# One-hot rows of the PEER gates: two tokens side by side in memory instead of four

## The chip, the core and the metric

The kernel runs on one core of a Trainium2 chip. The metric is the device time of one execution, in microseconds; the median of the runs shown counts. Every time below is from a run of this kernel or from one profiled execution of it.

TensorE (PE in the profile, its weight loads PEld) multiplies; VectorE (DVE) and ScalarE (ACT) do the elementwise work and empty the accumulators (PSUM banks, `bank` in the rows); GpSimd (POOL) helps; SyncE's queue (SPq) issues the transfers.

## The reference, cut to what matters

The network is a block with a recurrent mixer, a windowed attention and a mixture of experts, and behind it two layers of a second kind, each of which ends with PEER: 256 tokens, 16384 experts, eight heads that pick sixteen experts each. Only PEER is touched.

```python
def peer_ffn(x, wq, sub_keys, u_tab, v_tab):
    ...
    def block(xi):
        qv = (xi @ wq).reshape(B, PEER_BLOCK, PEER_HEADS, 2, half)
        s = jnp.einsum('bthpc,hpnc->bthpn', qv, sub_keys).astype(jnp.float32)
        top_s, top_i = lax.top_k(s, K)
        cand_s = (top_s[..., 0, :, None] + top_s[..., 1, None, :]).reshape(...)
        cand_i = (top_i[..., 0, :, None] * N_KEYS + top_i[..., 1, None, :]).reshape(...)
        best_s, best_j = lax.top_k(cand_s, K)
        expert = jnp.take_along_axis(cand_i, best_j, axis=-1)
        gate = jax.nn.softmax(best_s, axis=-1)
        act = jax.nn.gelu(jnp.einsum('btd,bthkd->bthk', xi, u_tab[expert]).astype(jnp.float32), approximate=False)
        return jnp.einsum('bthk,bthkd->btd', (gate * act).astype(xi.dtype), v_tab[expert])
```

An expert's number is n * 128 + m, two halves of 0 to 127. A token has 128 picks (8 heads of 16), each with a pair (n, m) and a gate.

## The kernel before

The kernel does not gather. For every token it computes gelu(u_e . x) of all 16384 experts and multiplies by a dense matrix of gates that is zero where an expert was not picked. `peer` has four parts.

*Queries and picks.* `pick` (line 2141) finds the picks of 128 tokens at a time. At its end (lines 2259 to 2262) TensorE transposes the four tables nn, mm, gh, gl (first half, second half, the gate in two float16 parts) into one PSUM bank, and ScalarE copies the bank into `picks`, float16, 128 picks on the partitions, as [4 tables, 256 tokens].

*Up.* `up` (line 2079) runs over 128 units of u. A unit is 128 experts: 24 matmuls of 256 columns in three float32r products (lines 418 to 420, `mm3`: high by high, low by high, high by low) into banks 0 to 2, then Gelu on ScalarE into B, [128, 128 units, 256 tokens]. Each unit's 512 KB arrive by a transfer on SyncE's queue; ScalarE splits off the high part (line 336), VectorE or GpSimd the low part (line 337, tile `wl`). While `pick` is busy on VectorE, units of `up` are put between its steps.

*Gating.* `gating` (line 2265) makes the gates, four tokens in a step, 64 steps in a layer. `hot` writes two float16 tiles of 128 x 1024 elements on VectorE. `e` (tile eq, line 2278) holds two one-hot tables: for each pick and each number 0 to 127, whether the pick's n (and m) is that number. `g` (tile gm, line 2279) is the one-hot of m multiplied by the gate's two parts. Then eight matmuls (line 2290), two for each token: weights are 128 numbers of one token of e, the moving columns 128 numbers of one token of g, summed over the 128 picks, so that a bank (of 3 to 6) gets the gates of 4 tokens. VectorE multiplies them into those units of B that are there (line 2292); for those that are still to come ScalarE stores the gates in B (line 2294), and `up` later applies them (lines 2086 to 2089). Both tiles have two buffers, and a step makes the tiles of the next one ahead.

*Down.* 128 units of v, matmuls of 512 columns (`down`, line 2119), accumulate in four banks.

Gating runs against `up`: `interleave` puts one step of the one behind one unit of the other, so that TensorE's queue holds 8 float16 matmuls and then 24 float32r ones, over and over. A scheduler in the framework sets each engine's final order from simulated times.

What the change touches is the order of the 1024 elements in a partition of eq and gm. Now the innermost index is the token, four side by side: the numbers 0, 1, 2, ... of one token stand 4 elements (8 bytes) apart, and that is the step with which TensorE reads both its weights and its columns at line 2290. VectorE reads `picks` in rows of four tokens, each repeated 128 times, and `iota16` (each number four times) in one run.

Of the kernel before, what the change touches and what calls it, by code (L numbers as in the profile page):

```python
# [12 lines left out]
F16 = mybir.dt.float16  # L13
U32 = mybir.dt.uint32
AF = mybir.ActivationFunctionType
OP = mybir.AluOpType
# [4 lines left out]
T = 256  # L21
# [319 lines left out]
def interleave(*gens):  # L341

    live = [[g, n] for g, n in gens]
    while live:
        for it in list(live):
            for _ in range(it[1]):
                try:
                    next(it[0])
                except StopIteration:
                    live.remove(it)  # L350
                    break
# [7 lines left out]
class Net:  # L359
# [1701 lines left out]
    def peer(self, l):  # L2061

        nc, tc, A, st = self.nc, self.tc, self.A, self.st
        with ExitStack() as es:
            pp = es.enter_context(tc.tile_pool(name="peer", bufs=1))
            B = pp.tile([128, 128, T], F32, name="B")
            picks = pp.tile([128, 4, T], F16, name="picks")
            hs = ExitStack()
            hp = hs.enter_context(tc.tile_pool(name="px", bufs=1))
            xh, xl = self.normal_t(hp, B[:, 64:72])  # L2070
            qT = B[:, 112:128].rearrange("p j t -> p (j t)").rearrange("p (j t) -> p j t", j=16)
            for j in range(16):
                ps = self.bank(0, 1)[:, :T]
                self.dense_t(ps, "wq", xh, xl)
                nc.scalar.copy(qT[:, j], ps)  # L2075

            at = dict(m=0, t=0)

            def up():

                for m in range(128):
                    ps = self.bank(0, 1, 2)[:, :T]
                    self.dense_t(ps, "pu", xh, xl)
                    t = at["t"]
                    if t < T:
                        nc.scalar.activation(B[:, m, t:], ps[:, t:], AF.Gelu)
                    if t:
                        nc.scalar.activation(ps[:, :t], ps[:, :t], AF.Gelu)
                        nc.vector.tensor_tensor(B[:, m, :t], B[:, m, :t], ps[:, :t], op=OP.mult)
                    at["m"] = m + 1  # L2090
                    yield

            ups = up()
            with tc.tile_pool(name="pk", bufs=1) as kp:
                st.pool_every = 3
                due = 0.0
                for us in self.pick(kp, l, B, qT, picks):
                    due += us
                    while due >= PICK_US:
                        due -= PICK_US  # L2100
                        next(ups)
            st.pool_every = 0
            with tc.tile_pool(name="pg", bufs=1) as pg:
                interleave((self.gating(pg, B, picks, at), 1), (ups, 1))
            st.pool_every = 0
            hs.close()
            pp = es.enter_context(tc.tile_pool(name="pv", bufs=1))
            acc = [self.ps[4 + b] for b in range(4)]
            self.settle(pp)
            parts = {}  # L2110

            def cut(m):
                parts[m] = [pp.tile([128, T], F32R, name=n, bufs=4) for n in ("gh", "gll")]
                self.split(*parts[m], B[:, m])

            cut(0)
            cut(1)

            def down(m, tt, gh, gl, wh, wl):
                t = slice(tt * 128, tt * 128 + 128)  # L2120
                for half in range(2):
                    c = slice(half * 512, half * 512 + 512)
                    ins = self.mm3(acc[tt * 2 + half], gh[:, t], gl[:, t], wh[:, c], wl[:, c], m == 0, m == 127)
                return ins

            for m in range(126):
                w = st.get("pv")
                cut(m + 2)
                for tt in range(2):
                    down(m, tt, *parts[m], *w)  # L2130
                del parts[m]
            st.hold = st.at + 2
            w = [st.get("pv") for _ in range(2)]

            down(126, 0, *parts[126], *w[0])
            with tc.issue_after(down(127, 0, *parts[127], *w[1]).ins):
                for j in range(2):
                    down(126 + j, 1, *parts[126 + j], *w[j])
            return [[(half, acc[tt * 2 + half]) for half in range(2)] for tt in range(2)]

    def pick(self, kp, l, B, qT, picks):
# [3 lines left out]
        nc, A = self.nc, self.A  # L2145
# [5 lines left out]
        def t(nm, shape, dt=F32, bufs=1):  # L2151
            if dt != F32:
                return kp.tile(shape, dt, name=nm, bufs=bufs)
            size = int(np.prod(shape[1:]))
            key = made.setdefault(nm, [used[0], 0])
            if not key[1]:
                used[0] += size * bufs
                assert used[0] <= 8192
            a = key[0] + key[1] % bufs * size
            key[1] += 1  # L2160
            ax = "abc"[:len(shape) - 1]
            return R[:, a:a + size].rearrange(f"p ({' '.join(ax)}) -> p {' '.join(ax)}", **dict(zip(ax, shape[1:])))
# [15 lines left out]
        for tt in range(2):  # L2178
# [32 lines left out]
            g = t("g", [128, 8, 16])  # L2211
# [17 lines left out]
            for h0 in range(0, 8, 4):  # L2229
                hs = slice(h0, h0 + 4)  # L2230
                big = [128, 4, 16, 15]
# [17 lines left out]
            for h0 in range(0, 8, 4):  # L2249
                big = [128, 16, 16]  # L2250
# [8 lines left out]
            pt = self.bank(3, 4)  # L2259
            for j, a in enumerate((nn, mm, gh, gl)):  # L2260
                nc.tensor.transpose(pt[:, j * 128:j * 128 + 128], a.rearrange("p h k -> p (h k)"), self.ident)
            nc.scalar.copy(picks[:, :, tt * 128:tt * 128 + 128], pt.rearrange("p (j t) -> p j t", j=4))
            yield 0.0

    def gating(self, pp, B, picks, at):


        nc = self.nc
        iota = pp.tile([128, 128, 4], F16, name="iota16")
        nc.vector.tensor_copy(iota, self.iota[:, :, None].to_broadcast([128, 128, 4]))  # L2270
        big = [128, 2, 128, 4]

        def hot(t0):

            e = pp.tile(big, F16, name="eq", bufs=2)
            g = pp.tile(big, F16, name="gm", bufs=2)
            of = lambda i: picks[:, i:i + 2, None, t0:t0 + 4].to_broadcast(big)
            nc.vector.tensor_tensor(e, iota[:, None].to_broadcast(big), of(0), op=OP.is_equal)  # L2278
            nc.vector.tensor_tensor(g, e[:, 1:2].to_broadcast(big), of(2), op=OP.mult)
            return e, g  # L2280

        made = {0: hot(0)}
        for t0 in range(0, T, 4):
            if t0 + 4 < T:
                made[t0 + 4] = hot(t0 + 4)
            e, g = made.pop(t0)
            ps = self.bank(3, 4, 5, 6).rearrange("p (t m) -> p m t", t=4)
            for j in range(4):
                for i in range(2):
                    nc.tensor.matmul(ps[:, :, j], e[:, 0, :, j], g[:, i, :, j], start=i == 0, stop=i == 1)  # L2290
            m, t = at["m"], slice(t0, t0 + 4)
            nc.vector.scalar_tensor_tensor(B[:, :m, t], B[:, :m, t], GATE_UNIT, ps[:, :m], op0=OP.mult, op1=OP.mult)
            if m < 128:
                nc.scalar.activation(B[:, m:, t], ps[:, m:], AF.Copy, scale=GATE_UNIT)
            at["t"] = t0 + 4
            yield
# [41 lines left out]
```

## Time and profile before

| | |
|---|---|
| median of 3 runs | 3211.7 us (3210.72 to 3220.12) |
| the profiled execution | 3216.49 us, its span 3214.7 us |
| granted TensorE clock, mean | 0.964 |
| TensorE busy | 3032.4 us, 94% of the span |
| VectorE, ScalarE, GpSimd busy | 2030.8, 1411.6, 374.5 us |
| gating, first layer | about 1405 to 1650 us of the span |
| gating, second layer | about 2589 to 2828 us |

A busy share is a mean over stages with different limits; what counts here is who is waited for in the two stretches of gating. A row of the timeline has start, length, engine, line, operation, what is written and read, and how many like it were merged; matmuls overlap, so the distance between starts tells what one costs, not its length. In the rows of one line, three numbers with slashes are the shortest, median and longest length in ns.

### The profile page before, as it was taken

To read this page: it belongs to the slowest core of one execution; us is meant where nothing else is said; L and a number is where in the kernel's file an instruction comes from. 1 tells how busy PE (TensorE), PEld (TensorE's weight loads), DVE (VectorE), ACT (ScalarE), POOL (GpSimd) and SP (SyncE) were. 2 spreads that over 40 slices of the span, in tenths; PEclk is the share of its full clock that TensorE was granted. 3 is DMA by queue.
4 is the path that set the end of the run, shared out by engine and by line. 5 is a ranking of instruction groups with operands and counts; after the bars stand their busy time and mean duration, and the time that the engine had idled before them with its cause. 6 is when DMAs were issued, how large, how long until landed. Compare 5 with 4: busy or idle time off the path is not lost. (4 is left out here: it accounts for less than half of the span.)

```text
span 3214.7 us, 52660 instructions
## 1 busy us (share of the span) xinstructions
PE 3032.4 (94%) x20690; PEld 2602.2 (81%) x20690; DVE 2030.8 (63%) x3822; ACT 1411.6 (44%) x2484; POOL 374.5 (12%) x334
## 2 busy tenths in 40 slices
PE   7999958899699989999999999999999999999998
PEld 5789647444488989999998888789899999988886
DVE  3568586211375578957876666664669667866666
ACT  4555433211254444444444545544454444444543
POOL 1110221000100222310010000110413300010000
PEclk9999968999899999999999999999999999999999
DMA  6323517699333444443445555533544544455564
GB/s 224 127 92 121 187 47 284 265 409 376 127 114 106 157 156 152 173 168 138 139 154 196 192 195 192 180 110 112 164 164 151 170 150 139 139 173 194 192 194 158
DMA packets 159134, 553.29 MB, mean 172 GB/s; under 512 B 19442, under 2 KB 25748, under 8 KB 157588
## 3 DMA queue, kind: packets, MB, share of 16 engines
q1 hardware_dynamic: 158868, 549.74, 49.4%
q8 instruction: 168, 2.75, 0.3%
q14 instruction: 98, 0.80, 0.1%
HBM read 548.62 MB, written 1.05 MB: 171 GB/s over the span
## 5 line engine op out<-in xcount | busy, mean ns | idle before, releaser
L337 DVE TENSOR_TENSOR wl<-wf,wh 128x1024 fp32r<-128x1024 f32 x690 | 870.8, 1262 | 409.9 <-ACT wh L336 409.3
L336 ACT CAST wh<-wf 128x1024 fp32r<-128x1024 f32 x745 | 779.3, 1047 | 708.3 <-PE bank L419 500.7
L418 PE MATMUL bank<-xth,wh 128*128 128x256 f32 x3040 | 886.5, 292 | 2.8 <-ACT B L2075 1.5
L420 PE MATMUL bank<-xth,wl 128*128 128x256 f32 x3040 | 870.4, 287 | 18.2 <-DVE wl L337 14.7
L419 PE MATMUL bank<-xtl,wh 128*128 128x256 f32 x3040 | 869.7, 286 | 0.7 <-DVE xtl L477 0.7
L420 PEld LDWEIGHTS bank<-xth,wl 128*128 128x128 f32 x3040 | 589.2, 194 | 22.2 <-DVE wl L337 16.9
L418 PEld LDWEIGHTS bank<-xth,wh 128*128 128x128 f32 x3040 | 591.7, 195 | 10.9 <-issue 1.9
L419 PEld LDWEIGHTS bank<-xtl,wh 128*128 128x128 f32 x3040 | 590.3, 194 | 1.9 <-DVE xtl L477 1.2
L419 PE MATMUL bank<-wl,gh 128*128 128x512 f32 x1024 | 399.8, 390 | 5.3 <-DVE wl L337 5.3
L420 PE MATMUL bank<-wh,gll 128*128 128x512 f32 x1024 | 397.5, 390 | 0.0
L418 PE MATMUL bank<-wh,gh 128*128 128x512 f32 x1024 | 279.1, 390 | 3.2 <-ACT gh L413 3.2
L413 ACT CAST gh<-B 128x256 fp32r<-128x256 f32 x256 | 103.6, 407 | 344.5 <-PE bank L419 344.5
L419 PEld LDWEIGHTS bank<-wl,gh 128*128 128x128 f32 x1024 | 192.8, 188 | 46.2 <-DVE wl L337 6.1
L418 PEld LDWEIGHTS bank<-wh,gh 128*128 128x128 f32 x1024 | 193.2, 189 | 43.9 <-ACT gh L413 3.6
L420 PEld LDWEIGHTS bank<-wh,gll 128*128 128x128 f32 x1024 | 192.9, 188 | 40.1
L414 DVE TENSOR_TENSOR gll<-B,gh 128x256 fp32r<-128x256 f32 x256 | 116.5, 457 | 132.2 <-ACT gh L413 129.6
L337 POOL TENSOR_TENSOR wl<-wf,wh 128x1024 fp32r<-128x1024 f32 (+1 forms) x55 | 148.4, 2701 | 321.2 <-ACT wh L336 321.2
L2278 DVE TENSOR_TENSOR eq<-iota,picks 128x1024 f16<-128x1024 f16 x128 | 89.5, 700 | 98.8 <-PE bank L2290 98.8
L2290 PE MATMUL bank<-gm,eq 128*128 128x128 f16 x1024 | 142.9, 296 | 0.0
L1445 PE MATMUL bank<-raw,xe 128*64 128x512 f32 x512 | 130.1, 600 | 0.0
L2290 PEld LDWEIGHTS <-eq 128*128 128x128 f16 x1024 | 103.6, 118 | 7.0
L506 POOL TENSOR_TENSOR x<-x,r_ln 128x1024 f32<-128x1024 f32 x12 | 33.0, 2783 | 552.3 <-DMA r_ln<-in_rows 540.9
(588 smaller groups left out, 4347.4 us busy)
## 6 DMA issues: line engine op xcount, KB each, us to landing
wf<-in_pu SPq DMA_DIRECT2D x256, 512.0 KB, 3.5
wf<-in_pv SPq DMA_DIRECT2D x256, 512.0 KB, 4.3
raw<-in_w SPq DMA_DIRECT2D x192, 512.0 KB, 10.2
wf<-in_mg SPq DMA_DIRECT2D x64, 512.0 KB, 3.5
mw<-in_modw SPq DMA_DIRECT2D x48, 512.0 KB, 4.5
wf<-in_win_t SPq DMA_DIRECT2D x37, 512.0 KB, 3.5
wf<-in_wq SPq DMA_DIRECT2D x32, 512.0 KB, 3.5
wf<-in_zt SPq DMA_DIRECT2D x28, 512.0 KB, 3.3
```

Source lines behind the costliest of these rows:

```text
L336: nc.scalar.copy(h[:, :w], src[:, :w])
L337: (nc.gpsimd if gpsimd else nc.vector).tensor_sub(lo[:, :w], src[:, :w], h[:, :w])
L413: self.nc.scalar.copy(h, src)
L414: return self.nc.vector.tensor_sub(lo, src, h)
L418: mm(out, lh, rh, start=start, stop=False)
L419: mm(out, lh, rl, start=False, stop=False)
L420: return mm(out, ll, rh, start=False, stop=stop)
L506: nc.gpsimd.tensor_tensor(self.x[:, tt], self.x[:, tt], gb[:, a:a + D], op=op)
L1445: nc.tensor.matmul(self.ps[j][half[e]], v[p]["x"][:, kk, half[e]], w[j][e][:, c], start=kk == 0, stop=kk == KC - 1)
L2278: nc.vector.tensor_tensor(e, iota[:, None].to_broadcast(big), of(0), op=OP.is_equal)
L2290: nc.tensor.matmul(ps[:, :, j], e[:, 0, :, j], g[:, i, :, j], start=i == 0, stop=i == 1)
```

## The change

Two tokens stand side by side instead of four. `e` and `g` become [2 pairs of tokens, 2 tables, 128 numbers, 2 tokens]: the numbers of a token now stand 2 elements (4 bytes) apart, and the four tokens of a step lie in two blocks of 512 elements. `picks` becomes [2 groups of tables, 128 pairs, 2 tables, 2 tokens], so that VectorE reads it in rows of two tokens, each repeated 128 times. `iota16` holds each number twice instead of four times. The instructions keep their number and their elements, but for the copy into `picks`: one ScalarE instruction of 512 elements becomes two of 256, four more in the whole program.

```diff
@@ peer
-            picks = pp.tile([128, 4, T], F16, name="picks")
+            picks = pp.tile([128, 2, T // 2, 2, 2], F16, name="picks")
@@ pick
-            nc.scalar.copy(picks[:, :, tt * 128:tt * 128 + 128], pt.rearrange("p (j t) -> p j t", j=4))
+            for i in range(2):
+                nc.scalar.copy(picks[:, i, tt * 64:tt * 64 + 64], pt[:, i * 256:i * 256 + 256].rearrange("p (j a t) -> p a j t", j=2, t=2))
@@ gating
-        iota = pp.tile([128, 128, 4], F16, name="iota16")
-        nc.vector.tensor_copy(iota, self.iota[:, :, None].to_broadcast([128, 128, 4]))
-        big = [128, 2, 128, 4]
+        iota = pp.tile([128, 128, 2], F16, name="iota16")
+        nc.vector.tensor_copy(iota, self.iota[:, :, None].to_broadcast([128, 128, 2]))
+        big = [128, 2, 2, 128, 2]
...
-            of = lambda i: picks[:, i:i + 2, None, t0:t0 + 4].to_broadcast(big)
-            nc.vector.tensor_tensor(e, iota[:, None].to_broadcast(big), of(0), op=OP.is_equal)
-            nc.vector.tensor_tensor(g, e[:, 1:2].to_broadcast(big), of(2), op=OP.mult)
+            of = lambda i: picks[:, i, t0 // 2:t0 // 2 + 2, :, None, :].to_broadcast(big)
+            nc.vector.tensor_tensor(e, iota[:, None, None].to_broadcast(big), of(0), op=OP.is_equal)
+            nc.vector.tensor_tensor(g, e[:, :, 1:2].to_broadcast(big), of(1), op=OP.mult)
...
-                    nc.tensor.matmul(ps[:, :, j], e[:, 0, :, j], g[:, i, :, j], start=i == 0, stop=i == 1)
+                    nc.tensor.matmul(ps[:, :, j], e[:, j // 2, 0, :, j % 2], g[:, j // 2, i, :, j % 2], start=i == 0, stop=i == 1)
```

The scheduler's order moves only where gating begins in the first layer. On TensorE, the eight float16 matmuls of the first step (one weight load and one matmul each) stood behind the last product of a unit (line 420 into bank 62 here). Before:

```order
L420 MATMUL bank_62<-xth,wl 128x256
L2290 LDWEIGHTS eq
L2290 MATMUL bank_64<-gm,eq 128x128
L2290 LDWEIGHTS eq
L2290 MATMUL bank_64<-gm,eq 128x128
```

Now (line 2292 is the old 2290) they begin between the second and the third product of that unit's first piece, 24 rows earlier:

```order
L419 MATMUL bank_62<-xtl,wh 128x256
L2292 LDWEIGHTS eq
L2292 MATMUL bank_64<-gm,eq 128x128
L2292 LDWEIGHTS eq
L2292 MATMUL bank_64<-gm,eq 128x128
```

The step's float16 work moved ahead of some 24 float32r matmuls; from the fifth step on the two orders agree. On VectorE, at the same place, the two gm tiles and the low part of a weight unit stood like this before:

```order
L2253 TENSOR_TENSOR B<-B,c_iota 128x256 x4
L337 TENSOR_TENSOR wl<-wf,wh 128x1024
L2279 TENSOR_TENSOR gm<-eq,picks 128x1024 x2
L2254 TENSOR_TENSOR B<-B 128x256 x4
L337 TENSOR_TENSOR wl<-wf,wh 128x1024
```

and now (2281 is the old 2279):

```order
L2253 TENSOR_TENSOR B<-B,c_iota 128x256 x4
L2281 TENSOR_TENSOR gm<-eq,picks 128x1024
L337 TENSOR_TENSOR wl<-wf,wh 128x1024
L2281 TENSOR_TENSOR gm<-eq,picks 128x1024
L2254 TENSOR_TENSOR B<-B 128x256 x4
```

One gm went ahead of the weight unit's low part. The second layer's gating keeps its order on every engine.

## Rows read from the trace of the kernel before

**Rows 1.** The page: span, engines, and the float16 matmuls' group.

```profile
span 3214.7 us, 52660 instructions
PE 3032.4 (94%) x20690; PEld 2602.2 (81%) x20690; DVE 2030.8 (63%) x3822; ACT 1411.6 (44%) x2484; POOL 374.5 (12%) x334
L2290 PE MATMUL bank<-gm,eq 128*128 128x128 f16 x1024 | 142.9, 296 | 0.0
```

**Rows 2.** Busy time of each engine in stretches of gating; the sum is of five.

```profile
core 0: us, PE busy (x) PEld busy (x) DVE busy (x) ACT busy (x) POOL busy (x), PEclk, DMA share, GB/s
...
1600.00:1650.00 50.00, 50.00 (x420) 49.29 (x420) 41.53 (x64) 20.81 (x53) 0.00 (x0) 1.00 0.41 141
...
2750.00:2800.00 50.00, 50.00 (x421) 49.28 (x419) 41.88 (x67) 22.42 (x52) 0.00 (x0) 1.00 0.43 139
sum 230.00, PE 230.00 PEld 226.70 DVE 184.42 ACT 98.88 POOL 0.00; mean PE 46.00 PEld 45.34 DVE 36.88 ACT 19.78 POOL 0.00
```

**Rows 3.** The chain that ended last, second layer's gating: start, length, what.

```profile
2704.12 0.95 PE bank L2290 x8
2707.94 0.95 PE bank L2290 x8
```

**Rows 4.** Timeline of TensorE around one step's eight float16 matmuls.

```profile
1418.51 0.28 PE L419 MATMUL bank<-xtl,wh 128*128 128x256 f32 x1
1418.63 0.28 PE L420 MATMUL bank<-xth,wl 128*128 128x256 f32 x1
1418.75 1.11 PE L2290 MATMUL bank<-gm,eq 128*128 128x128 f16 x8
1419.62 0.37 PE L418 MATMUL bank<-xth,wh 128*128 128x256 f32 x1
1419.82 0.28 PE L419 MATMUL bank<-xtl,wh 128*128 128x256 f32 x1
```

**Rows 5.** Timeline of TensorE in "down": matmuls of 512 columns.

```profile
1899.63 0.39 PE L418 MATMUL bank<-wh,gh 128*128 128x512 f32 x1
...
1900.99 0.39 PE L420 MATMUL bank<-wh,gll 128*128 128x512 f32 x1
```

**Rows 6.** Lengths by line on TensorE and its weight loads (shortest/median/longest ns).

```profile
L2290 PEld LDWEIGHTS <-eq x1024: 110/117/146, 1358.2 to 2827.5; 128*128 128x128 f16 x171
L2290 PE MATMUL bank<-gm,eq x1024: 283/297/323, 1358.2 to 2827.6; 128*128 128x128 f16 x171
...
L420 PEld LDWEIGHTS bank<-xth,wl x3040: 186/192/338, 871.3 to 2847.2; 128*128 128x128 f32 x190
L420 PE MATMUL bank<-xth,wl x3040: 277/283/679, 871.4 to 2847.3; 128*128 128x256 f32 x190
...
L420 PE MATMUL bank<-wh,gll x1024: 387/389/628, 1673.0 to 3201.7; 128*128 128x512 f32 x171
...
L554 PEld LDWEIGHTS bank<-mw,sc x128: 106/109/177, 323.4 to 442.6; 128*32 128x32 f32 x128
```

**Rows 7.** Timeline of VectorE in gating, in brackets idle time before and its releaser.

```profile
1542.29 0.69 DVE L2278 TENSOR_TENSOR eq<-iota,picks 128x1024 f16<-128x1024 f16 x1 [0.74 <-PE bank L2290]
...
1545.09 0.29 DVE L2089 TENSOR_TENSOR B<-B,bank 128x140 f32<-128x140 f32 x1
1546.12 0.69 DVE L2278 TENSOR_TENSOR eq<-iota,picks 128x1024 f16<-128x1024 f16 x1 [0.73 <-PE bank L2290]
...
2808.36 0.69 DVE L2278 TENSOR_TENSOR eq<-iota,picks 128x1024 f16<-128x1024 f16 x1 [0.55 <-PE bank L2290]
```

**Rows 8.** Lengths by line on VectorE, float32, two inputs.

```profile
L1905 DVE TENSOR_TENSOR blk<-zT,cpos x2: 991/992/994, 938.8 to 2111.8; 128x480 f32<-128x480 f32 x2
...
L1207 DVE TENSOR_TENSOR y<-y,hst x2: 680/682/685, 512.8 to 520.9; 128x512 f32<-128x512 f32 x2
...
L2253 DVE TENSOR_TENSOR B<-B,c_iota x32: 398/411/419, 1305.0 to 2535.8; 128x256 f32<-128x256 f32 x32
```

**Rows 9.** Length of the copy into the picks, ScalarE.

```profile
L2262 ACT CAST picks<-bank x4: 576/576/578, 1325.6 to 2572.4; 128x512 f16<-128x512 f32 x4
```

## The prediction

> **What bounds the kernel now.** I read the page first: TensorE is busy 94% of the span and its 1024 float16 matmuls of line 2290 stand there as one group [rows 1]. A share over the whole span does not say who is waited for while they run, so the next view is the busy time of the engines in stretches of gating [rows 2]: TensorE is busy in every microsecond of the five stretches (230.00 of 230.00 us), VectorE in 184.42 (80%), ScalarE in 98.88, GpSimd in none, the granted clock is 1.00, its upper level. The chain that ended last says the same: it runs on TensorE through the second layer's gating and counts each step's eight float16 matmuls with 0.95 us, a step every 3.82 to 3.83 us [rows 3]; the first layer's gating is not in it, but its stretches are just as full [rows 2]. So in gating time is what TensorE issues, and one nanosecond less for each float16 matmul is one microsecond less for the kernel, as long as VectorE keeps up.
>
> What one costs is read from starts, since lengths overlap. The last float32r matmul ahead of the eight starts at 1418.63, the second behind them at 1419.82 [rows 4]: 1.19 us, less two ordinary intervals of 0.12 (1418.51 to 1418.63, same rows), leaves 0.95, as the chain has it: **0.119 us for a matmul of 128 columns**. A float32r matmul of 256 columns costs 0.120 [rows 4], one of 512 costs 0.227 (six intervals from 1899.63 to 1900.99) [rows 5]. The two float32r prices lie on a line: 0.107 us for 256 columns and 0.013 fixed. On it 128 columns would cost 0.053 + 0.013 = 0.067. The float16 matmul pays as if it had 256 columns. Its recorded length says so too: 297 ns, where 256 columns of float32r take 283 and 512 take 389 [rows 6].
>
> What is different in it is the step: a float32r operand goes 4 bytes from column to column, the float16 one 8. 128 columns by 8 bytes span the same 1024 bytes as 256 by 4. The price follows the bytes spanned, and the change halves those.
>
> **The change part by part.**
>
> *The matmuls (line 2290), columns and weights at 4 bytes.* With the columns read as float32r's are, the interval is 0.067 us and the gain 1024 x (0.119 - 0.067) = 53 us. The bounds: at best the fixed part goes as well, 0.053, a gain of 67 us; at worst nothing, if the step is not what is paid for. Between them I take 0.067, since two rows of this kernel give both its parts. The weight load must not become the next bound: a load of 32 columns is recorded with 109 ns, one of 128 float32r columns with 192 [rows 6], so 0.86 ns a column over some 81 that overlap; the float16 load's 117 stands for some 42 columns, about 36 ns of its own, under 67.
>
> A page has a rule against this. The Trainium skill, "SBUF — State Buffer", section "Door 1: The DMA port swizzle", says that memory is read in lines of 16 bytes and that two hits on a line are enough for the full rate. An 8-byte step has two hits on a line, so by this rule the columns already come at full rate and the change gives 0 in place of 53 us. No row here shows float16 at another step; that the interval fits 256 float32r columns speaks against the rule. It is the first rival.
>
> *VectorE's two tiles (lines 2278, 2279).* Elements and instructions stay; rows of two tokens, each repeated, replace rows of four. The eq instruction takes 0.69 us for 1024 elements [rows 7]; float32 with two inputs takes 411 ns for 256 elements and 682 for 512 [rows 8], 1.06 ns an element over 140 fixed, so eq and gm already make two elements in the time of one. A pair is one 4-byte word and the row still holds a pair: I take 0. What a repeated word costs is seen at line 2253, which reads each float32 word 16 times on end: 411 ns for 256 elements; line 1207, which repeats each word 64 times, has the same rate. The row against it is line 1905, whose words lie 64 bytes apart: 992 ns for 480 elements, where 140 + 480 x 1.06 = 649 would do, so 0.71 ns for a word that is hopped to [rows 8]. The changed read returns to the same word, so it is nearer to lines 2253 and 1207. Bounds: 0 and 512 x 0.71 = +0.37 us an instruction, both above zero, since nothing about these instructions gets shorter; pairing lost is a rival.
>
> The Trainium skill, "Vector Engine (DVE) Microarchitecture Reference", section "5.2 Measured stream behaviour on trn2", asks for runs of at least two neighbouring 4-byte words for the full rate; a row of two float16 is one word, a row of four was two. Line 1905 agrees with it, lines 2253 and 1207 show that a repeat is not a hop. By the rule to the letter the two instructions cost the 0.37 us above each, and the sum is that of the second rival's milder form.
>
> *Does VectorE keep up?* Its busy share of 0.802 times 3.825 us is 3.07 us a step [rows 2]. With TensorE's step at 3.825 - 8 x 0.052 = 3.41 there is room on the mean. Late in a layer it waits 0.55 us of a step for the matmuls to free the eq tile [rows 7], so 0.42 less leaves 0.13: still TensorE's step. eq waits for the release of a buffer that is needed one step later (two buffers), so a late eq does not at once stop TensorE. Queued behind it on VectorE are wl, the gates' product of line 2292, gm and line 2089; the next units' matmuls wait for wl, two units ahead. ScalarE, at 98.88 of 230 us, has room [rows 2].
>
> *The copies into picks.* One of 576 ns [rows 9] becomes two. Bounds: half the length each (0), and each the whole length (+0.58 us); four times in all, so 0 to +2.3 us. ScalarE waits at that stage and TensorE is full, so 0; without that cover, 2.3.
>
> *The order.* It moves only in the first layer's first steps, ahead of the steady stretch. There one group of eight (0.95 us now) stands 24 rows earlier and one gm goes ahead of one wl. If TensorE came to wait for them it would be for one gm or wl; the bound is one gm of 0.69 us [rows 7] either way, -0.7 to +0.7. I take 0. The few steps made while VectorE is full with picking give their gain to its wait: three or four of 128, some 1.5 us.
>
> *Sum.* -53 + 1.5 = about -52 us. It stands against the profiled execution, 3216.5 us, of which 3214.7 are span: 3164.5. That execution was 4.8 us above the median of the runs, 3211.7; the same gain off the median gives **3160 us**.
>
> **The rivals.**
>
> *The step is not what is paid.* Then the float16 matmul waits for something else, the weight load first of all: it is recorded with 117 ns and the interval is 119. If a matmul cannot begin before its load is finished, the interval only falls towards the 32-column load's 109 [rows 6]: 1024 x 0 to 0.010 = 0 to 10 us, 3202 to 3212. For it: how near 117 and 119 are. Against it: float32r loads are recorded with 192 ns at an interval of 120, so there a load's length does not set the pace; and the matmul's own 297 ns. The rule of the page on lines ends here too.
>
> *VectorE becomes the bound: slower.* If a row of two is too short for the pairing, eq and gm go one element at a time: 140 + 1024 x 1.06 = 1225 ns in place of 0.69 us, +0.53 each, +1.07 a step. VectorE's 3.07 become 4.14 and it sets the step, 0.31 over the 3.825 of now: 128 x 0.31 = +40 us, **3252 us**. The point from which it decides is 3.41 us of VectorE's work a step, so +0.34, and slower than before from +0.76. The milder form, 0.37 us for a hop at each word, gives 3.81, just the step of now: 3210, no change. For it: the row of four is what the tiles have now, and line 1905. Against it: lines 2253 and 1207.
>
> *Part of it.* A part of the 0.119 follows the step and a part does not, or VectorE's last steps bind: intervals of 0.080 to 0.110, a gain of 9 to 40 us, 3172 to 3203. Nothing in the rows asks for it, but the weights' read moves with the same step, and what loads and columns share is not seen.
>
> That the change does not do what it says: the step stands in the matmul's operands, so the 4 bytes are read for certain; what may not follow is the price, which is the first rival.
>
> **How the numbers follow.** The forecast, an interval of 0.053 to 0.080: 60%, 3145 to 3172, with 3160 in it. Part of it: 12%, 3172 to 3203. No change, the first rival and the milder form of the second: 18%, 3202 to 3221. VectorE the bound: 10%, up to 3252. The range holds the first case but its last few microseconds, the second, and the part of the third that ends under 3207: 3148 to 3207, about 8 in 10. A measurement of this kernel can tell 0.3%, some 10 us, from no change: faster by more has the first two cases and a bit of the third, 74%; within it 16%; slower 10%.
>
> **What would show it.** In the changed kernel's trace: the chain's piece of eight float16 matmuls falls from 0.95 to about 0.53 us and the steps' distance from 3.82 to 3.41; the recorded length falls from 297 to some 230 ns (283 less half of 107). If the piece stays at 0.85 to 0.95, the first rival is right. eq and gm stay at 0.69 us; 1.2 shows lost pairing, 1.05 a hop at each word. VectorE's wait for line 2290 shrinks from 0.55 to 0.74 to some 0.1 to 0.3 us a step; TensorE waiting for eq, gm or wl inside the stretches would make the sum wrong even with the matmuls right.

## The result, and the profile after

The changed kernel takes **3162.6 us** (median of four runs, 3153.6 to 3167.7) where the kernel before took 3215.0 in the runs beside it (four, 3210.7 to 3220.1): a ratio of **0.983, 95% interval 0.981 to 0.985**, 52.4 us less. The forecast was 52 us less, 3160 us.

The page of the changed kernel first: span, engines, and the group of eq's tile. Its profiled execution took 3153.6 us, the fastest of the four, so its span lies below the median.

```profile
span 3151.8 us, 52665 instructions
PE 2972.6 (94%) x20690; PEld 2544.3 (81%) x20690; DVE 2028.2 (64%) x3822; ACT 1411.4 (45%) x2488; POOL 382.0 (12%) x334
...
L2280 DVE TENSOR_TENSOR eq<-iota,picks 128x1024 f16<-128x1024 f16 x128 | 89.4, 699 | 47.1 <-PE bank L2292 45.7
```

Compared with [rows 1], TensorE is busy 60 us less, with as many matmuls, and its share is 94% as before: it still sets the pace, with less to do. VectorE's busy time is the same within 3 us. The float16 matmuls (line 2292 now) have dropped out of the page's list of costliest groups.

The chain that ended last in the second layer's gating, one step from its eight float16 matmuls to the next (start, length, what):

```profile
2643.58 0.48 PE bank L2292 x8
2644.06 0.17 PE bank L418
2644.23 0.12 PE bank L419
...
2646.98 0.48 PE bank L2292 x8
```

The piece of eight is 0.48 us in place of 0.95 [rows 3], the float32r matmul behind it 0.17 where the others have 0.12, and the step is 3.40 us in place of 3.82. That is 0.42 us a step, and 128 steps make 54 us.

The timeline of TensorE around one step's eight (start, length, engine, line):

```profile
1521.68 0.28 PE L420 MATMUL bank<-xth,wl 128*128 128x256 f32 x1
1521.80 0.63 PE L2292 MATMUL bank<-gm,eq 128*128 128x128 f16 x8
1522.24 0.36 PE L418 MATMUL bank<-xth,wh 128*128 128x256 f32 x1
1522.44 0.28 PE L419 MATMUL bank<-xtl,wh 128*128 128x256 f32 x1
```

Read as [rows 4] were: from 1521.68 to 1522.44 is 0.76 us, less two ordinary intervals of 0.12 leaves 0.52 for eight, **0.065 us each** (0.119 before). The merged row tells the interval inside the group as well: it is 0.63 us long, and without the last matmul's own 0.22 that is 0.41 for seven intervals, 0.059 each. In [rows 4] the same reading gives (1.11 - 0.30) / 7 = 0.116.

Lengths by line, shortest/median/longest ns: the weight loads and matmuls of line 2292, VectorE's two tiles, ScalarE's copies into the picks.

```profile
L2292 PEld LDWEIGHTS <-eq x1024: 95/97/101, 1350.7 to 2766.7; 128*128 128x128 f16 x171
L2292 PE MATMUL bank<-gm,eq x1024: 217/218/233, 1350.7 to 2766.7; 128*128 128x128 f16 x171
...
L2280 DVE TENSOR_TENSOR eq<-iota,picks x128: 674/692/1627, 1346.5 to 2759.9; 128x1024 f16<-128x1024 f16 x128
...
L2281 DVE TENSOR_TENSOR gm<-eq,picks x128: 671/685/1773, 1349.1 to 2762.6; 128x1024 f16<-128x1024 f16 x128
...
L2263 ACT CAST picks<-bank x8: 362/374/385, 1320.2 to 2538.7; 128x256 f16<-128x256 f32 x8
```

The gm tile in the kernel before:

```profile
L2279 DVE TENSOR_TENSOR gm<-eq,picks x128: 676/684/692, 1355.0 to 2822.7; 128x1024 f16<-128x1024 f16 x128
```

Against [rows 6] the matmul's length fell from 297 to 218 ns and the load's from 117 to 97. VectorE's two tiles are where they were, eq at 0.69 us as in [rows 7] and gm at 685 ns after 684. The copies cost ScalarE 8 x 374 - 4 x 576 [rows 9], 0.7 us in the whole program, with nothing waiting for it.

Busy time in stretches of gating, one in each layer:

```profile
core 0: us, PE busy (x) PEld busy (x) DVE busy (x) ACT busy (x) POOL busy (x), PEclk, DMA share, GB/s
1420.00:1620.00 200.00, 200.00 (x1885) 197.51 (x1883) 179.19 (x291) 99.78 (x237) 0.00 (x0) 1.00 0.45 156
2580.00:2760.00 180.00, 180.00 (x1696) 177.72 (x1696) 162.97 (x266) 90.24 (x212) 0.00 (x0) 1.00 0.48 155
sum 380.00, PE 380.00 PEld 375.23 DVE 342.15 ACT 190.03 POOL 0.00; mean PE 190.00 PEld 187.62 DVE 171.08 ACT 95.01 POOL 0.00
```

TensorE is busy throughout, as in [rows 2], at the upper clock level as before. VectorE went from 80% to 90% (342.15 of 380): 0.90 x 3.40 = 3.06 us a step, the 3.07 of before in a shorter step. How little room is left is seen in VectorE's timeline (idle time before in brackets), in the middle of the first layer and near the end of the second:

```profile
1522.47 0.69 DVE L2280 TENSOR_TENSOR eq<-iota,picks 128x1024 f16<-128x1024 f16 x1 [0.32 <-PE bank L2292]
...
2735.90 0.69 DVE L2280 TENSOR_TENSOR eq<-iota,picks 128x1024 f16<-128x1024 f16 x1 [0.16 <-PE bank L2292]
...
2742.18 0.38 DVE L2089 TENSOR_TENSOR B<-B,bank 128x220 f32<-128x220 f32 x1
2742.70 0.69 DVE L2280 TENSOR_TENSOR eq<-iota,picks 128x1024 f16<-128x1024 f16 x1
```

The wait at about the same place in the layer was 0.74 and is 0.32; near the layer's end it is 0.16, and two steps later 0.14 (2742.18 + 0.38 to 2742.70). In the steady steps of both layers its wait before eq never falls under 0.11 us: VectorE still waits for TensorE in each of them, but barely.

*Where the time went.* I matched the matmuls of the two traces by their number and followed the distance of their starts. Ahead of the first gating the two executions already stood 5 us apart, drift that has nothing to do with the edit; the first layer's gating brought it to 34, next to nothing came in the 890 us between, and the second layer's gating and its end brought it to 63. So the two gatings are worth 28 to 29 us each, 57 together. The profiled executions differ by 63 us: the one of the changed kernel was the fastest of its set and that of the kernel before was not. By the medians it is 52, and the interval of the ratio reaches from 49 to 61 us, so that the 57 of this one pair of executions is no contradiction.

### The profile page after: what moved, and what is told of

It reads as the page before. It is cut to its first block, busy times and chain, and to the rows that moved or that the text cites. A ratio compares the mean times of both kernels' runs of the same rounds, so it can differ in the third digit from the quotient of the medians.

```text
span 3151.8 us, 52665 instructions
## 1 busy us (share of the span) xinstructions
PE 2972.6 (94%) x20690; PEld 2544.3 (81%) x20690; DVE 2028.2 (64%) x3822; ACT 1411.4 (45%) x2488; POOL 382.0 (12%) x334
## 5 line engine op out<-in xcount | busy, mean ns | idle before, releaser
L1445 PEld LDWEIGHTS bank<-raw,xe 128*64 128x64 f32 x512 | 37.2, 136 | 66.0 <-issue 64.2
L2281 DVE TENSOR_TENSOR gm<-eq,picks 128x1024 f16<-128x1024 f16 x128 | 88.6, 693 | 0.0
```

The lines of the kernel that those rows point to most:

```text
L1445: nc.tensor.matmul(self.ps[j][half[e]], v[p]["x"][:, kk, half[e]], w[j][e][:, c], start=kk == 0, stop=kk == KC - 1)
L2281: nc.vector.tensor_tensor(g, e[:, :, 1:2].to_broadcast(big), of(1), op=OP.mult)
```

## The experiments

**The theory**: the float16 matmul pays for its columns by the bytes from one to the next, and nothing else in the change matters. **The rivals**: the weight load sets the pace, through the weights' step; or part of the gain comes from VectorE's tiles, the copies or the order. Five kernels change only the operands at line 2292 of the changed kernel and leave tiles, copies and order as they are. They read a tile flat, as one row of 1024 elements, at the step that is to be tested, and so multiply other elements than the gates need; what they measure is time. In the diffs below, `flat` stands for the flat read, which the kernels write out, and only the new line is shown from the second on.

### Both operands back at 8 bytes

```diff
-nc.tensor.matmul(ps[:, :, j], e[:, j // 2, 0, :, j % 2], g[:, j // 2, i, :, j % 2], ...)
+flat = lambda a: a.rearrange("p a k n t -> p (a k n t)")[:, 512 * i + j:512 * i + j + 509:4]
+nc.tensor.matmul(ps[:, :, j], flat(e), flat(g), ...)
```

> The changed kernel, but line 2292 reads both its weights and its columns at a step of 8 bytes again, from the same tiles: the elements it multiplies are the wrong ones, and all else (VectorE's rows of two, the copies into picks, the order) is the changed kernel's. If the step alone is what was paid, the kernel before comes back: 0.95 us for a step's eight matmuls, 3.82 us a step, 3215 us. If VectorE's layout, the copies or the order had a part in it, the time lies between 3163 and 3215 us by that part.

Measured: 3216.6 us (ten runs), ratio to the kernel before 0.9996 [0.9984, 1.0008]. The lengths at line 2292:

```profile
L2292 PEld LDWEIGHTS <-eq x1024: 111/117/136, 1359.7 to 2828.8; 128*128 128x128 f16 x171
L2292 PE MATMUL bank<-gm,eq x1024: 283/297/301, 1359.7 to 2828.9; 128*128 128x128 f16 x171
```

These are [rows 6] again, 117 and 297, and the steps are 3.82 us apart. With the whole of the change in place but for the step of the operands, nothing is gained and nothing lost: VectorE's rows of two, the copies and the order are together worth 0 within 5 us (the interval's 0.16% of 3216).

### The columns alone at 8 bytes

```diff
+nc.tensor.matmul(ps[:, :, j], e[:, j // 2, 0, :, j % 2], flat(g), ...)
```

> The changed kernel with the columns at 8 bytes and the weights at 4 (the columns multiplied are the wrong ones). Theory, the columns pay: interval 0.119 us, steps 3.82 us apart, recorded length some 290 ns, time 3215 us. Rival, the weight load pays (its recorded length fell from 117 to 97 ns with the change): interval 0.058, 3163 us. If both reads share one limit: in between, some 0.09 us and 3190 us.

Measured: 3214.5 us (ten runs), ratio 0.9996 [0.9986, 1.0007]. The lengths at line 2292:

```profile
L2292 PEld LDWEIGHTS <-eq x1024: 96/115/119, 1357.7 to 2829.9; 128*128 128x128 f16 x171
L2292 PE MATMUL bank<-gm,eq x1024: 274/296/300, 1357.7 to 2830.0; 128*128 128x128 f16 x171
```

TensorE's timeline, two groups of eight:

```profile
1520.12 1.09 PE L2292 MATMUL bank<-gm,eq 128*128 128x128 f16 x8
...
1523.92 1.10 PE L2292 MATMUL bank<-gm,eq 128*128 128x128 f16 x8
```

The step is 3.80 to 3.81 us: weights at 4 bytes with columns at 8 give no gain that can be measured. The weights' step is not what was paid for. The load is recorded with 115 ns here, although its weights stand at 4 bytes as in the changed kernel, where it is 97. So a load's recorded length moves with the columns' step too, and does not tell what the load costs.

### The weights alone at 8 bytes

```diff
+nc.tensor.matmul(ps[:, :, j], flat(e), g[:, j // 2, i, :, j % 2], ...)
```

> The changed kernel with the weights at 8 bytes and the columns at 4 (the weights multiplied are the wrong ones). Theory, the columns pay: interval 0.058 us, 3163 us, the load's recorded length back at some 110 to 117 ns. Rival, the weight load pays: interval 0.119 us, steps 3.82 us apart, 3215 us. If both reads share one limit: some 0.09 us and 3190 us.

Measured: 3165.7 us (four runs), ratio 0.985 [0.983, 0.987]. Lengths at line 2292:

```profile
L2292 PEld LDWEIGHTS <-eq x1024: 111/113/136, 1353.1 to 2773.8; 128*128 128x128 f16 x171
L2292 PE MATMUL bank<-gm,eq x1024: 217/221/251, 1353.1 to 2773.8; 128*128 128x128 f16 x171
```

TensorE's timeline, two groups of eight:

```profile
1521.87 0.66 PE L2292 MATMUL bank<-gm,eq 128*128 128x128 f16 x8
...
1525.30 0.67 PE L2292 MATMUL bank<-gm,eq 128*128 128x128 f16 x8
```

The load is recorded with 113 ns, in place of 97, and the interval inside a group is (0.67 - 0.22) / 7 = 0.064 us: a matmul does not wait for the recorded length of its load. The step is 3.43 us in place of 3.40: 0.03 x 128 = 4 us for the weights, which the comparison of whole runs can't tell from nothing. Together with the run before it: the columns' step is all of the gain that can be measured.

### Both operands at 16 bytes

```diff
+flat16 = lambda a: a.rearrange("p a k n t -> p (a k n t)")[:, 2 * j + i:2 * j + i + 1017:8]
+nc.tensor.matmul(ps[:, :, j], flat16(e), flat16(g), ...)
```

> The changed kernel with weights and columns at a step of 16 bytes, 128 of each across the whole tile (the elements multiplied are the wrong ones). Theory, the price follows the bytes that the columns span: twice that of 8 bytes, 0.213 us of reading and an interval of 0.22 to 0.23, 1.8 us for a step's eight, 4.7 us a step, some 3320 us. If the price stops growing at 8 bytes: 0.119 us and 3215 us.

Measured: 3337.4 us (one run). Lengths at line 2292:

```profile
L2292 PEld LDWEIGHTS <-eq x1024: 142/146/173, 1357.0 to 2948.2; 128*128 128x128 f16 x171
L2292 PE MATMUL bank<-gm,eq x1024: 406/413/436, 1357.0 to 2948.4; 128*128 128x128 f16 x171
```

TensorE's timeline around one group:

```profile
1518.71 0.28 PE L420 MATMUL bank<-xth,wl 128*128 128x256 f32 x1
1518.83 2.06 PE L2292 MATMUL bank<-gm,eq 128*128 128x128 f16 x8
...
1520.85 0.28 PE L419 MATMUL bank<-xtl,wh 128*128 128x256 f32 x1
```

From 1518.71 to 1520.85, less 0.24, is 1.90 for eight, 0.237 each; inside the group (2.06 - 0.41) / 7 = 0.236. The interval doubles with the step: 0.059, 0.116, 0.236 at 4, 8 and 16 bytes; 0.22 to 0.23 and 3320 us were expected. The recorded load (146) is far from it, but weights and columns were not taken apart at 16 bytes, as they were at 8.

### Both operands side by side, 2 bytes

```diff
+flat2 = lambda a: a.rearrange("p a k n t -> p (a k n t)")[:, (2 * j + i) * 128:(2 * j + i) * 128 + 128]
+nc.tensor.matmul(ps[:, :, j], flat2(e), flat2(g), ...)
```

> The changed kernel with weights and columns in one run, a step of 2 bytes (the elements multiplied are the wrong ones). If the price goes on following the bytes spanned, the interval falls from 0.058 us towards 0.03 and the kernel by another 28 us, to 3135. If at 4 bytes the columns already stream at their own rate (0.053 for 128, by the slope of the float32r rows), it stays at 0.058 and the time at 3163 us.

Measured: 3157.9 us (four runs), ratio 0.982 [0.980, 0.984], which overlaps that of the changed kernel. TensorE's timeline around one group:

```profile
1521.48 0.28 PE L420 MATMUL bank<-xth,wl 128*128 128x256 f32 x1
1521.60 0.62 PE L2292 MATMUL bank<-gm,eq 128*128 128x128 f16 x8
...
1522.23 0.28 PE L419 MATMUL bank<-xtl,wh 128*128 128x256 f32 x1
```

Eight cost 0.75 - 0.24 = 0.51 us, where they cost 0.52 at 4 bytes; the steps are 3.38 us apart. So of the two outcomes the second came: from 4 bytes down to 2 the price of a column hardly falls.

### One token in a row

This kernel makes the layout with 2 bytes for TensorE in earnest, and multiplies the right elements: each VectorE row is one token, repeated 128 times. It tests the slower rival, that the row becomes too short for two elements at a time.

```diff
-            picks = pp.tile([128, 2, T // 2, 2, 2], F16, name="picks")
+            picks = pp.tile([128, 2, T, 2], F16, name="picks")
...
-        iota = pp.tile([128, 128, 2], F16, name="iota16")
-        big = [128, 2, 2, 128, 2]
+        iota = pp.tile([128, 128], F16, name="iota16")
+        big = [128, 4, 2, 128]
...
-            of = lambda i: picks[:, i, t0 // 2:t0 // 2 + 2, :, None, :].to_broadcast(big)
+            of = lambda i: picks[:, i, t0:t0 + 4, :, None].to_broadcast(big)
...
+                    nc.tensor.matmul(ps[:, :, j], e[:, j, 0], g[:, j, i], start=i == 0, stop=i == 1)
```

> One token in a row instead of two: a step of 2 bytes for TensorE, and VectorE reads each pick alone, 128 times on end, in a row of one. The slower rival's mechanism: VectorE's pairing is lost, eq and gm take 1.2 us each in place of 0.69, VectorE's work a step is 3.06 + 1.06 = 4.1 us and sets the step: 3163 + 128 x 0.7 = some 3255 us, TensorE waiting for eq and gm or for wl. If a repeated element keeps the pairing: 0.69 us, 3163 us as after the change.

Measured: 3235.2 us (four runs), ratio to the kernel before 1.006 [1.004, 1.008]: slower than before. Lengths of the two tiles and of the matmuls:

```profile
L2280 DVE TENSOR_TENSOR eq<-iota,picks x128: 1210/1217/3421, 1353.6 to 2844.5; 128x1024 f16<-128x1024 f16 x128
...
L2281 DVE TENSOR_TENSOR gm<-eq,picks x128: 1208/1217/2233, 1358.3 to 2847.1; 128x1024 f16<-128x1024 f16 x128
...
L2292 PE MATMUL bank<-gm,eq x1024: 219/219/230, 1361.2 to 2850.6; 128*128 128x128 f16 x171
```

VectorE's timeline for one step, and a row of TensorE's there with its wait in brackets:

```profile
1521.86 1.23 DVE L2280 TENSOR_TENSOR eq<-iota,picks 128x1024 f16<-128x1024 f16 x1
1523.00 1.22 DVE L337 TENSOR_TENSOR wl<-wf,wh 128x1024 fp32r<-128x1024 f32 x1
1524.13 0.27 DVE L2089 TENSOR_TENSOR B<-B,bank 128x108 f32<-128x108 f32 x1
1524.31 1.22 DVE L2281 TENSOR_TENSOR gm<-eq,picks 128x1024 f16<-128x1024 f16 x1
...
1525.87 1.22 DVE L2280 TENSOR_TENSOR eq<-iota,picks 128x1024 f16<-128x1024 f16 x1
...
1524.45 0.38 PE L418 MATMUL bank<-xth,wh 128*128 128x256 f32 x1 [0.40 <-DVE B L2089]
```

The matmuls are as cheap as they get (219 ns), and it is lost elsewhere: eq and gm take 1217 ns each, VectorE has no wait left before eq, and TensorE waits 0.40 us a step for line 2089, which queues behind wl and eq. So the bound moved. The step is 4.01 us here (1521.86 to 1525.87), 3.9 early in a layer and 4.3 at its end, since lines 2089 and 2294 take more columns as the layer goes on. The expectation counted 0.7 us of loss for all 128 steps and came out 20 us too high. Following the distance of the matmuls' starts to the changed kernel's, as above, the first dozen steps of each layer lose nothing: the distance stays at 14 to 15 us from 1418 to 1446 of the changed kernel's span, and at 43 from 2573 to 2601. TensorE's first wait of this kind comes at 1465 here, and at 2643 in the second layer. From there on each layer loses 36 us, some 0.7 a step as expected. A dozen steps in each of two layers at 0.7 are 17 us. Where picking still runs there are small shifts beside this, 8 us lost in the first layer and 4 gained in the second. So the first steps are most of the miss, as far as one pair of executions can tell.

### Half the float16 matmuls

The low part of the gates is left out, so each step has four float16 matmuls in place of eight, at 4 bytes. It measures what a float16 matmul costs now, and when VectorE takes over.

```diff
-                for i in range(2):
-                    nc.tensor.matmul(ps[:, :, j], e[...], g[:, j // 2, i, :, j % 2], start=i == 0, stop=i == 1)
+                nc.tensor.matmul(ps[:, :, j], e[...], g[:, j // 2, 0, :, j % 2], start=True, stop=True)
```

> The changed kernel without the gates' low part: four float16 matmuls a step instead of eight, all else the same. If TensorE still sets the step after the change: 3.40 - 4 x 0.065 = 3.14 us a step, 128 x 0.26 = 33 us less, 3130 us. If VectorE is already the limit: the step stays near 3.4 us and the time near 3163; VectorE's work of 3.06 us on the mean and some 3.27 in the last steps would take a few us of the 33 back.

Measured: 3142.7 us (four runs), ratio to the kernel before 0.977 [0.975, 0.979]; against the changed kernel's 3162.6 it is 20 us less, where 33 were expected. Busy time in two stretches of the first layer (columns as above):

```profile
1430.00:1560.00 130.00, 130.00 (x1150) 128.28 (x1149) 123.33 (x201) 66.68 (x165) 0.00 (x0) 1.00 0.50 168
1570.00:1616.00 46.00, 42.64 (x365) 40.84 (x364) 40.99 (x65) 20.28 (x52) 0.00 (x0) 1.00 0.45 150
```

The timeline late in that layer, rows of TensorE over a pair of steps and one of VectorE's:

```profile
1591.03 0.39 PE L418 MATMUL bank<-xth,wh 128*128 128x256 f32 x1 [0.55 <-DVE B L2089]
1593.90 0.40 PE L2291 MATMUL bank<-gm,eq 128*128 128x128 f16 x4
1594.67 0.40 PE L2291 MATMUL bank<-gm,eq 128*128 128x128 f16 x4
1598.20 0.39 PE L418 MATMUL bank<-xth,wh 128*128 128x256 f32 x1 [0.57 <-DVE B L2089]
...
1594.34 0.63 DVE L2293 SCALAR_TENSOR_TENSOR B<-B,bank 128x456 f32<-128x456 f32 x1 [0.72 <-PE bank L2291]
```

Early in a layer the steps with 24 float32r matmuls are 3.17 us apart, 0.23 under the changed kernel's 3.40: four matmuls less are worth 0.057 each, the interval inside the group, not the 0.065 that also holds what is paid once behind a group, since each group still pays that. That is 0.03 us a step, 4 us of the 13 missing. Late in the layer the order is another one: the scheduler, working from its own estimate of times, put two steps' groups close together (1593.90 and 1594.67, then 7.2 us to the next pair), so VectorE waits 0.72 us for the pair and TensorE then 0.55 for VectorE. There are eight such pairs in each layer. Over the whole of them TensorE is busy 56.77 of 61 us (1555 to 1616) and 57.77 of 62 (2695 to 2757), so it is idle 4.2 us in each layer, 8.5 in both. With the 4 us above this makes some 12 of the 13.

## Why the prediction was right

**What bounds the kernel: right.** TensorE was busy in every microsecond of the stretches, and 0.42 us less in each of 128 steps, 54 us, is the whole gain within the spread of the runs. The columns-alone kernel, with the same VectorE work, has the old step back.

**The price of the matmul, 0.119 to 0.067: right in size, 0.065 measured, its make-up a little off.** The line through the two float32r widths gave 0.053 for 128 columns and 0.013 fixed per matmul. Measured inside a group is 0.059; the rest is paid once per group, where float32r begins again behind it (0.17 in place of 0.12 in the chain). The forecast put the fixed part into every matmul, and it is luck that eight of them add up to nearly the same: 8 x 0.067 = 0.54, measured 0.52. The half kernel, with four, told the two readings apart.

**"The price follows the bytes spanned": right at 4, 8 and 16 bytes, wrong as a law.** 0.059, 0.116 and 0.236 follow the step; 2 bytes cost nearly as much as 4, 0.057. The forecast needed only the first two. By the law the kernel with 2 bytes would have taken 3135 us, and it took 3157.9: a forecast for that halving would have been 23 us too low.

**The weight load, first rival: excluded.** It was near by number alone, 117 beside 119. With the columns at 8 bytes the interval stayed though the weights' step was halved, and with the weights at 8 bytes the load was recorded with 113 ns while the interval was 0.064 us. The forecast's reason against it, a float32r load of 192 ns beside an interval of 0.12 us, holds. Its estimate that the float16 load has only some 36 ns of its own is not shown: it was worked out from recorded lengths, and these move with the columns' step as well (115 ns in the columns-alone kernel, 97 in the changed one). No run measured the load by itself.

**The rule on lines, the same rival: the trace disagrees.** The Trainium skill, "SBUF — State Buffer", "Door 1: The DMA port swizzle", says that two hits on a 16-byte line are enough for the full rate. For TensorE's columns that would put 8 bytes on a par with 4. They cost 0.116 and 0.059 us here, and the measurement decides.

**eq and gm, 0: right.** They take 692 and 685 ns, as they did before, and the kernel with both operands at 8 bytes stands at the time of before. A repeated 4-byte word cost nothing here. The Trainium skill, "Vector Engine (DVE) Microarchitecture Reference", section "5.2 Measured stream behaviour on trn2", asks for two neighbouring 4-byte words for the full rate. Here rows of one word, repeated, took no longer (692 ns) than rows of two words (0.69 us in [rows 7]), so for a repeated word the trace disagrees.

**VectorE keeps up: right.** The forecast left 0.13 us of wait late in the layer; the rows show 0.16 and 0.14, the smallest wait is 0.11, and mid-layer it is 0.32 where there was 0.74.

**The slower rival: a true mechanism, one halving further on.** One token in a row lost the pairing at once: 1217 ns, where the forecast had 1225, and the kernel came out slower than before by 0.6%. Its price for this kernel was 20 us too high (3235, not 3255), mostly because the first dozen steps of each layer lost nothing, so a price by VectorE's mean work is an upper bound. At rows of two it doesn't come.

**Small terms.** The copies cost 374 ns each and nobody waited. The order moved as shown and its worth is within the 5 us of the kernel with both operands at 8 bytes. Whether the first steps lost the 1.5 us of the forecast is below what can be told.

## What to carry to other kernels

Read a matmul's price from starts and set it beside one of another type whose columns span the same bytes: if a narrow type costs as much as a wide one, look at its step before its size. Bring the moving operand of a 2-byte type, the columns, to a step of 4 bytes. In these runs 2 bytes gained hardly more, and the weights' step hardly counted. When the layout is made by an element-wise engine, keep pairs side by side for it: here rows of two serve both engines, rows of one cost VectorE more than TensorE gains.

## What the runs showed of the hardware

- A float16 matmul of 128 columns, in a train of its like, costs 0.057 us with both operands at a step of 2 bytes ((0.62 - 0.22) / 7), 0.059 at 4, 0.116 at 8 and 0.236 at 16. At 4 and 8 bytes it is the columns' step that decides.
- The weights' step, 8 bytes in place of 4, costs 0.03 us in eight matmuls. The recorded length of the load does not tell this: it is 97 ns with both operands at 4 bytes, 113 with only the weights at 8, 115 with only the columns at 8, 117 with both at 8 and 146 with both at 16.
- Behind a group of float16 matmuls at 4 bytes, 0.05 us is paid once, beside the price of each matmul (0.52 less 8 x 0.059). The same reading leaves 0.02 at 8 bytes (0.95 less 8 x 0.116 [rows 4]) and 0.01 at 16. What it is stays open: the change to float32r itself, or the float32r weight load, recorded with 192 ns [rows 6], which one short matmul may not cover.
- VectorE's float16 comparison of 1024 elements takes 692 ns with an operand whose rows are two elements, each row repeated 128 times, and 1217 ns where each row is a single element so repeated.
